# The attention softmax's scale moved into the query rows, its maximum written negated, and logits and transposes asked for one weight unit sooner

## The chip, the core and the metric

The kernel runs on one core of a Trainium2 chip. A core has a matrix engine (TensorE, PE in the profile, with its weight loads as PEld), two engines for rows of numbers (VectorE, DVE; ScalarE, ACT), GpSimd (POOL) and a queue that only starts transfers (SyncE, SP). They run side by side, each through its own list of instructions, and wait for each other by semaphores. PE writes into PSUM, a small memory of sums; the others work between PSUM and SBUF. The metric is the device time of one launch in microseconds (us), as the median of several runs.

## The reference

One layer of a streaming encoder over 256 rows of 2048 numbers, all in 32-bit floats: a feed-forward half step, a mixer, attention on 256 memory rows, a second feed-forward half step, a last norm. The change touches the attention alone:

```python
def mem_cross_attention(h, mem_h, w_q, w_kv, w_o):
    q = (h @ w_q).reshape(b, s, XATTN_HEADS, XATTN_HEAD_DIM)
    kv = (mem_h @ w_kv).reshape(b, mem_h.shape[1], 2, XATTN_HEADS, XATTN_HEAD_DIM)
    k, v = kv[:, :, 0], kv[:, :, 1]
    logits = jnp.einsum('bshd,bmhd->bhsm', q, k).astype(jnp.float32) * (XATTN_HEAD_DIM ** -0.5)
    p = jax.nn.softmax(logits, axis=-1).astype(v.dtype)
    o = jnp.einsum('bhsm,bmhd->bshd', p, v).reshape(b, s, D_MODEL)
    return o @ w_o
```

There are 4 heads of 512 columns. `h` and `mem_h` are the normed rows (each row by the root of its mean square, times a gain).

## The kernel before

**Numbers in two parts.** Every operand of a product is split into a high part in the format that PE multiplies (`fp32r`) and the rest: the high part is a cast on ACT, the low part a subtraction on DVE. A product is then three matmuls: high by high, high by low, low by high (`products`). Activations lie split in `xs` and `ys`.

**Weights stream.** Weights come from memory in units of 1 MB (a tile `raw`, three buffers, loaded on SP's queue at L627). ACT casts the high part `wh` (L1582), DVE subtracts the low part `wl` (L453; a share of some units goes to POOL, L457); each has three buffers. The class `Stream` holds the list of units with their matmuls. Before the matmuls of a unit it asks for the split of the unit two further on; the load of `raw` follows when the split of the third unit before it has given the buffer back. Other work is put between units with `st.op(f, after)`: `f` is asked for when `after` more units have been put in the list. A planner then sets the final order on each engine from its own idea of times, so an op that is asked for sooner is not always placed sooner.

**Blocks.** `block_s` makes 1024 columns for 256 rows from eight units. A plain unit is 24 matmuls of 512 columns (L362). Some units are taken in pairs of row and column halves with seven products in place of eight, 21 matmuls (`seven`, L507). For these the split is another: sums `T` of the weights on DVE (L486), their casts `wh` (L489) and rest `wl` (L453), and casts and rest `xh`, `xl` of the raw weights (L279, L280). The buffers of `T`, `xh` and `xl` are lent by other tiles of the stage (`homes`); in the key and value blocks `xh` and `xl` live in the tiles `att` and `kv`, and the latter is also the home of the split keys and values.

A block with seven-product units needs four tiles of sums in PSUM, and PSUM has just four (`psum`, `bufs=4`, two banks each): two for the whole sums, which every unit adds to, and two "parts" tiles for sums that only the seven-product units make, called A (first and sixth product) and B (seventh and fifth) here. In the profile all four are named `pt`, as are the tiles of the probabilities' transposes. At the last seven-product unit the parts are added up on ACT and DVE (`combine`, L574 to L579), at the block's end they go into the whole sums (L589).

**The attention stage.** Two blocks make the queries (`w_q`), and `ev_Q` multiplies the rows by the norm's factor `Rcol` on ACT before they are turned (`turn_Q`). Then twice, for two heads each: a block for the keys, turned and split by `turn_K`, and a block for the values. The unit order of a value block is (1, 5, 3, 0, 6, 4, 2, 7): the fourth, sixth and seventh unit are seven-product units, the others plain. The softmax of the two heads lies inside this value block:

- `logits(h)`: 24 matmuls into a PSUM tile `pl` (L1321), the rows' maximum on DVE (L1327), times minus the scale (L1328), for two halves of rows the exponential on ACT with its row sums (L1331), the reciprocal of the sums (L1335) and the scaling of the probabilities `P` by it (L1337), both on DVE.
- `probs(h)`: four transposes of `P` on PE into a PSUM tile (L1343), split into `PT` by ACT (L285) and DVE (L286).
- `values(h)`: at the block's end, 48 matmuls for two heads (L1360).

So while the value block holds its two whole sums, the other two PSUM tiles pass from the logits of the two heads to the two heads' transposes and then to A and B. The output projection (`into_x` with `w_o`) follows behind the second value block. The lines that ask for the softmax stand between the key block and the value block:

```python
        for j in (1, 0):
            h = 2 * b + j
            st.op(lambda h=h: turn_K(h), 1)
        for h in (2 * b, 2 * b + 1):
            st.op(lambda h=h: logits(h), 2)
            st.op(lambda h=h: probs(h), 3)
        block_s(wwide(w_kv, D + b * 2 * NB), xs, kv_sums, KV_ORDER, ev_V(b))
```

The functions that the change touches, with the line numbers of the profile:

Of the kernel before, what the change touches and what calls it, by code (L numbers as in the profile page):

```python
# [9 lines left out]
AF = mybir.ActivationFunctionType  # L10
ALU = mybir.AluOpType
AX = mybir.AxisListType
PSUM = bass.MemoryType.PSUM

P = 128
D = 2048
S = 256
M = 256
# [8 lines left out]
XHD = D // H  # L27
# [72 lines left out]
def build(ctx, tc, I, out):  # L100
    nc = tc.nc
    st = Stream()
# [34 lines left out]
    def ptile(name):  # L137
        return psum.tile([P, 2, NB], F32, tag="ps", name=name)
# [6 lines left out]
    def uid(s):  # L145
        cnt[0] += 1
        return f"{s}{cnt[0]}"
# [9 lines left out]
    def whole_lines(pool, shape, dt, tag, name, bufs=1):  # L157

        n = 1
        for s in shape[1:]:  # L160
            n *= s
        t = pool.tile([shape[0], -(-n // LINE) * LINE], dt, tag=tag, name=name, bufs=bufs)[:, :n]
        if len(shape) == 3:
            t = t.rearrange("p (a b) -> p a b", b=shape[2])
        elif len(shape) == 4:
            t = t.rearrange("p (a b c) -> p a b c", b=shape[2], c=shape[3])
        return t

    def ctl(name, shape):
        return whole_lines(const, shape, F32, name, name)  # L170
# [10 lines left out]
    Rcol = ctl("Rcol", [P, 2])  # L181
# [88 lines left out]
    def among_weights(f):  # L270


        scalar, vector = behind_weights(f)
        latest["vector"] = vector
        if scalar is not None:
            latest["scalar"] = scalar
# [7 lines left out]
    def split(hi, lo, src):  # L284
        high = nc.scalar.copy(hi, src)  # L285
        return high, nc.vector.tensor_tensor(out=lo, in0=src, in1=f32(hi), op=ALU.subtract)  # L286

    def split_pair(dst, kt, src):
        split(dst[:, kt : kt + 2, 0, :], dst[:, kt : kt + 2, 1, :], src)
# [349 lines left out]
    def wwide(w, n0, k0=0, nk=KT):  # L639

        def src(k):
            def load(raw):
                raw = raw.rearrange("p (k n) -> p k n", n=2 * NB)
                if len(loaded) < 3:
                    for kk in range(2):
                        parts = (0, NB) if not loaded else (0,)
                        for c in parts:
                            n = 2 * NB // len(parts)
                            wload(raw[:, kk : kk + 1, c : c + n], w, k + kk, 1, n0 + c, n)
                else:  # L650
                    wload(raw, w, k, 2, n0, 2 * NB)
                next(first_loads, None)
                loaded.append(1)
            return load
        return [src(k0 + k) for k in range(0, nk, 2)]
# [557 lines left out]
    for b in range(2):  # L1213
        block_b(wblock(w_in, (4 + b) * NB), xs, ev_v(b))
        for i in range(2):
            h = 2 * b + i
# [24 lines left out]
    xa = {}  # L1241

    def xt(name, shape, dt=F32, tag=None, bufs=1):
        t = whole_lines(scope["pool"], shape, dt, tag or name, uid(name), bufs)
        xa[name] = t
        return t
# [46 lines left out]
    def ev_Q(b):  # L1293
        def evict(j, c):
            for h in range(2):
                nc.scalar.activation(c[:, h, :], c[:, h, :], AF.Copy, scale=Rcol[:, h : h + 1])
            held["Q", b, j] = c
        return evict

# [4 lines left out]
    def turn_K(h):  # L1304
        v = rows_turned(held["K", h])
        K = xa["K", h] = xt("K", [P, 4, 2, M], F32R, tag="kv", bufs=2)
        split(K[:, :, 0, :], K[:, :, 1, :], v)

    def ev_V(b):
        def evict(j, c):  # L1310
            V = xa["V", 2 * b + j] = xt("V", [P, 2, 2, XHD], F32R, tag="kv", bufs=2)
            split(V[:, :, 0, :], V[:, :, 1, :], c)
        return evict

    def logits(h):
        ps = ptile(uid("pl"))
        for t in range(2):
            tok = slice(t * P, (t + 1) * P)
            parts = [(d, a, b) for d in range(4) for a, b in ((0, 0), (0, 1), (1, 0))]
            for i, (d, a, b) in enumerate(parts):  # L1320
                nc.tensor.matmul(  # L1321
                    ps[:, t, :M], ys[:, 4 * h + d, a, tok], xa["K", h][:, d, b, :],
                    start=i == 0, stop=i == 11,
                )
        scale = XHD ** -0.5
        nm, sm = xt("nm", [P, 2], bufs=2), xt("sm", [P, 2], bufs=2)
        nc.vector.tensor_reduce(out=nm, in_=ps[:, :, :M], axis=AX.X, op=ALU.max)  # L1327
        nc.vector.tensor_scalar_mul(nm, nm, -scale)  # L1328
        pr = xa["P", h] = xt("P", [P, 2, M], bufs=2)
        for t in range(2):  # L1330
            nc.scalar.activation(  # L1331
                pr[:, t, :], ps[:, t, :M], AF.Exp, scale=scale, bias=nm[:, t : t + 1],
                accum_out=sm[:, t : t + 1],
            )
        nc.vector.reciprocal(out=sm, in_=sm)  # L1335
        for t in range(2):
            nc.vector.tensor_scalar_mul(pr[:, t, :], pr[:, t, :], sm[:, t : t + 1])  # L1337

    def probs(h):
        ps = ptile(uid("pt"))  # L1340
        for mtile in range(2):
            for t in range(2):
                nc.tensor.transpose(  # L1343
                    ps[:, mtile, t * P : (t + 1) * P], xa["P", h][:, t, mtile * P : (mtile + 1) * P], ident
                )
        if h % 2 == 0:
            xt("PT", [P, D], F32R)
        PT = xa["PT", h] = xa["PT"][:, h % 2 * 4 * S : (h % 2 + 1) * 4 * S].rearrange(
            "p (m a s) -> p m a s", m=2, a=2
        )  # L1350
        split(PT[:, :, 0, :], PT[:, :, 1, :], ps[:, :, :S])

    def values(h):
        for p in range(2):
            ps = ptile(uid("pv"))
            for d in range(2):
                col = slice((2 * p + d) * P, (2 * p + d + 1) * P)
                parts = [(m, a, b) for m in range(2) for a, b in ((0, 0), (0, 1), (1, 0))]
                for i, (m, a, b) in enumerate(parts):
                    nc.tensor.matmul(  # L1360
                        ps[:, d, :S], xa["V", h][:, m, a, col], xa["PT", h][:, m, b, :],
                        start=i == 0, stop=i == 5,
                    )
            split_pair(ys, 4 * h + 2 * p, ps[:, :, :S])

    for g, after in zip(q_sums.pairs, (3, 7)):
        st.op(lambda g=g: among_weights(lambda: q_sums.make(g)), after)
    for b in range(2):
# [9 lines left out]
    for b in range(2):  # L1378
        block_s(wwide(w_kv, b * 2 * NB), xs, kv_sums, KV_ORDER if b else KEY_ORDER,
                lambda j, c, b=b: held.__setitem__(("K", 2 * b + j), c),  # L1380
                sevens=() if b else (0, 4))
        for j in (1, 0):
            h = 2 * b + j
            st.op(lambda h=h: turn_K(h), 1)
        for h in (2 * b, 2 * b + 1):
            st.op(lambda h=h: logits(h), 2)
            st.op(lambda h=h: probs(h), 3)
        block_s(wwide(w_kv, D + b * 2 * NB), xs, kv_sums, KV_ORDER, ev_V(b))
        for h in (2 * b, 2 * b + 1):
            st.op(lambda h=h: values(h), 1)  # L1390
# [211 lines left out]
def program(shapes):  # L1602
    import concourse.bacc as _bacc

    nc = _bacc.Bacc("TRN2", target_bir_lowering=False, num_devices=1)
    args = {
        name: nc.dram_tensor(f"in_{name}", shapes[name], F32, kind="ExternalInput").ap()
        for name in _INS
    }
    out = nc.dram_tensor("out", _OUT, F32, kind="ExternalOutput").ap()  # L1610
    with tile.TileContext(nc, schedule_with_timeline_sim=True) as tc, ExitStack() as ctx:
        build(ctx, tc, args, out)
    return nc
# [10 lines left out]
```

## Time and profile before

| | |
|---|---|
| runs | 2086.03, 2086.88, 2087.07 us; median 2086.88 |
| profiled execution | 2086.24 us, span of the trace 2084.1 us |
| granted TensorE clock | 0.999 |
| busy in the span | PE 2069.3, weight loads 1724.8, DVE 1800.0, ACT 1143.4, POOL 98.6 us |
| busy from 1100 to 1200 us | PE 98.50, DVE 83.02, ACT 52.15 us |
| busy from 1200 to 1300 us | PE 98.48, DVE 77.83, ACT 48.17 us |
| busy from 1300 to 1400 us | PE 100.00, DVE 83.48, ACT 57.31 us |
| logits' matmuls (L1321) | 96, first 1149.1, last 1255.8 us |
| probabilities' transposes (L1343) | 16, first 1161.5, last 1270.7 us |

How to read it. Matmuls overlap each other, and their ends are worked out by the profiler and not seen, so their durations (0.39 us for 512 columns) add up to more than the time that passes; what counts is the distance from one start to the next. In a time line, a row stands for one or more like instructions in a run, with the start of the first, the time to the end of the last, the engine, the line, the tile written and those read, and the count; in square brackets how long the engine stood idle before it and what ended that. In a list of waits, a row names the waiting engine, tile and line, what it waited for, and then the total in us, how many times, and the longest.

### The profile page before, as it was taken

How to read it: one execution, taken by the hardware profiler on the slowest of the kernel's cores; microseconds unless marked ns; L12 is line 12 of the kernel's file. 1: busy time of each engine (PE TensorE's matmuls, PEld its weight loads, DVE VectorE, ACT ScalarE, POOL GpSimd, SP SyncE). 2: the span in 40 equal slices, each digit the busy share in tenths (PEclk: the TensorE clock that was granted, in tenths of full speed). 3: DMA queues.
4: the chain of work that ended last, by engine and by line, in shares of the span. 5: the costliest groups of instructions: out<-in, count | busy, mean ns of one | idle time of the engine just before them, and what ended most of it. 6: DMA issues, size and time to landing. Idle time of an engine off the chain costs nothing.

```text
span 2084.1 us, 24353 instructions
## 1 busy us (share of the span) xinstructions
PE 2069.3 (99%) x9651; PEld 1724.8 (83%) x9651; DVE 1800.0 (86%) x1689; ACT 1143.4 (55%) x1136; POOL 98.6 (5%) x87
## 2 busy tenths in 40 slices
PE   9999999999999999999999999999999999999998
PEld 7888888888888888888888888888888888888886
DVE  7998899989998677679789787879988999889987
ACT  7655455645654545455755554556554556545554
POOL 0000000000000000000000000000100010000001
PEclk9999999999999999999999999999999999999999
DMA  7666666567656755467655455665576765676664
GB/s 264 208 200 229 232 222 222 182 222 243 223 200 221 245 164 185 159 192 275 220 181 189 155 182 172 211 224 202 182 241 207 240 206 196 222 238 227 208 228 150
DMA packets 131178, 435.95 MB, mean 209 GB/s; under 512 B 9844, under 2 KB 13528, under 8 KB 130680
## 3 DMA queue, kind: packets, MB, share of 16 engines
q1 hardware_dynamic: 130888, 433.86, 61.8%
q8 instruction: 76, 1.25, 0.2%
q10 hardware_dynamic: 176, 0.53, 0.1%
q14 instruction: 38, 0.31, 0.0%
HBM read 417.58 MB, written 16.78 MB: 208 GB/s over the span
## 4 chain that ended last, share of the span: by engine, by line
PE 98%; DVE 1%; ACT 0%; issue 0%; DMA 0%; SPq 0%; DVEq 0%; ACTq 0%
PE pt L362 58%; PE pt L507 27%; PE pa L347 6%; PE pb L362 2%; PE ph L780 1%; DVE wl L453 1%; PE pl L1321 1%; PE pv L1360 1%; PE px L791 1%; PE pp L1012 0%; PE pe L362 0%; DMA x<-in_x 0%; ACT wh L1582 0%; ACT wh L489 0%; PE pa L1039 0%
## 5 line engine op out<-in xcount | busy, mean ns | idle before, releaser
L362 PE MATMUL pt<-wh,xs 128*128 128x512 f32 x2080 | 666.6, 390 | 0.6 <-ACT xs L236 0.6
L453 DVE TENSOR_TENSOR wl<-raw,wh 128x2048 fp32r<-128x2048 f32 (+1 forms) x253 | 545.2, 2161 | 138.4 <-ACT wh L1582 138.0
L1582 ACT CAST wh<-raw 128x2048 fp32r<-128x2048 f32 x253 | 483.4, 1913 | 301.5 <-PE pt L362 126.7
L362 PE MATMUL pt<-wh,ys 128*128 128x512 f32 x1472 | 463.9, 389 | 0.0
L489 ACT CAST wh<-T 128x1024 fp32r<-128x1024 f32 x242 | 254.1, 1054 | 373.9 <-DVE T L486 361.6
L362 PEld LDWEIGHTS pt<-wh,xs 128*128 128x128 f32 x2080 | 389.8, 188 | 80.8 <-ACT xs L236 0.9
L362 PE MATMUL pt<-wl,xs 128*128 128x512 f32 x1040 | 405.4, 391 | 2.3 <-DVE wl L453 2.3
L362 PEld LDWEIGHTS pt<-wh,ys 128*128 128x128 f32 x1472 | 276.3, 188 | 57.0
L362 PE MATMUL pt<-wl,ys 128*128 128x512 f32 x736 | 286.7, 390 | 0.0
L453 DVE TENSOR_TENSOR wl<-T,wh 128x2048 fp32r<-128x2048 f32 (+1 forms) x121 | 271.6, 2245 | 2.9 <-ACT wh L489 2.6
L362 PEld LDWEIGHTS pt<-wl,xs 128*128 128x128 f32 x1040 | 195.3, 188 | 43.0 <-DVE wl L453 3.1
L280 DVE TENSOR_TENSOR xl<-raw,xh 128x1536 fp32r<-128x1536 f32 x121 | 211.9, 1752 | 13.7 <-ACT xh L279 13.5
L279 ACT CAST xh<-raw 128x1536 fp32r<-128x1536 f32 x121 | 179.0, 1480 | 54.9 <-PE pt L507 35.7
L486 DVE TENSOR_TENSOR T<-T,raw 128x512 f32<-128x512 f32 x242 | 167.0, 690 | 6.2
L362 PEld LDWEIGHTS pt<-wl,ys 128*128 128x128 f32 x736 | 138.2, 188 | 28.6
L486 DVE TENSOR_TENSOR T<-raw 128x1024 f32<-128x1024 f32 x121 | 147.5, 1219 | 0.5
L507 PE MATMUL pt<-wh,xs 128*128 128x512 f32 x376 | 145.8, 389 | 0.0
L507 PE MATMUL pt<-xh,xs 128*128 128x512 f32 x376 | 140.8, 390 | 0.0
L457 POOL TENSOR_TENSOR wl<-raw,wh 128x768 fp32r<-128x768 f32 x40 | 74.3, 1857 | 1380.0 <-DVE wl L453 1358.9
L347 PE MATMUL pa<-xs,wh 128*128 128x512 f32 x384 | 135.6, 397 | 0.0
L507 PE MATMUL pt<-wh,xe 128*128 128x512 f32 x320 | 124.3, 389 | 0.0
L347 PE MATMUL pa<-xs,wl 128*128 128x256 f32 x384 | 106.8, 282 | 0.0
(248 smaller groups left out, 2343.8 us busy)
## 6 DMA issues: line engine op xcount, KB each, us to landing
raw<-in_ffn_w_down SPq DMA_DIRECT2D x88, 1024.0 KB, 5.5
raw<-in_ffn_w_up SPq DMA_DIRECT2D x80, 1024.0 KB, 5.0
raw<-in_ffn_w_gate SPq DMA_DIRECT2D x77, 1024.0 KB, 5.0
raw<-in_w_in SPq DMA_DIRECT2D x32, 1024.0 KB, 5.2
raw<-in_xattn_w_kv SPq DMA_DIRECT2D x32, 1024.0 KB, 5.0
raw<-in_w_out SPq DMA_DIRECT2D x16, 1024.0 KB, 5.6
raw<-in_xattn_w_q SPq DMA_DIRECT2D x16, 1024.0 KB, 5.6
raw<-in_xattn_w_o SPq DMA_DIRECT2D x16, 1024.0 KB, 5.6
```

Of the source, the lines that this page charges most:

```text
L279: in_turn("scalar", lambda: nc.scalar.copy(hi, src))
L280: in_turn("vector", lambda: nc.vector.tensor_tensor(out=lo, in0=src, in1=f32(hi), op=ALU.subtract))
L347: nc.tensor.matmul(o, w, x, start=k == 0 and i == 0, stop=last and i == 1)
L362: nc.tensor.matmul(ps, a, w, start=first and i == 0, stop=last and i == 2)
L453: in_turn("vector", lambda: nc.vector.tensor_tensor(out=lo[:, :n], in0=src[:, :n], in1=f32(hi[:, :n]), op=ALU.subtract))
L457: rest = nc.gpsimd.tensor_tensor(out=lo[:, n:], in0=src[:, n:], in1=f32(hi[:, n:]), op=ALU.subtract)
L486: in_turn("vector", lambda: nc.vector.tensor_tensor(out=o, in0=a, in1=b, op=ALU.add))
L489: in_turn("scalar", lambda: nc.scalar.copy(th[:, c], t[:, c]))
L507: nc.tensor.matmul(banks[n], x, w, start=n in fresh and j == 0, stop=n in ends and j == 2)
L780: nc.tensor.transpose(v[:, i, h * P : (h + 1) * P], g[:, h, i * P : (i + 1) * P], ident)
L791: nc.tensor.transpose(v[:, j, h * P : (h + 1) * P], x[:, h, j * P : (j + 1) * P], ident)
L1582: in_turn("scalar", lambda: nc.scalar.copy(hi, raw))
```

## The change

Three edits in the attention stage.

- The scale of the softmax, 512 to the power of minus one half, goes into the query rows: a new op `query_factor`, asked for three units into the first query block, writes `Rq`, the norm's factor times the scale, with one product on DVE (128 x 2). `ev_Q` multiplies by `Rq` where it took `Rcol`. The exponentials take the logits unscaled.
- The reduce writes the negated maximum itself (`negate=True`), and the product that made it so is gone: one instruction of DVE for each of 4 heads.
- `logits` is asked for after one unit of the value block in place of two, `probs` after two in place of three.

```diff
     def ev_Q(b):
         def evict(j, c):
             for h in range(2):
-                nc.scalar.activation(c[:, h, :], c[:, h, :], AF.Copy, scale=Rcol[:, h : h + 1])
+                nc.scalar.activation(c[:, h, :], c[:, h, :], AF.Copy, scale=xa["Rq"][:, h : h + 1])
             held["Q", b, j] = c
...
-        scale = XHD ** -0.5
         nm, sm = xt("nm", [P, 2], bufs=2), xt("sm", [P, 2], bufs=2)
-        nc.vector.tensor_reduce(out=nm, in_=ps[:, :, :M], axis=AX.X, op=ALU.max)
-        nc.vector.tensor_scalar_mul(nm, nm, -scale)
+        nc.vector.tensor_reduce(out=nm, in_=ps[:, :, :M], axis=AX.X, op=ALU.max, negate=True)
         pr = xa["P", h] = xt("P", [P, 2, M], bufs=2)
         for t in range(2):
             nc.scalar.activation(
-                pr[:, t, :], ps[:, t, :M], AF.Exp, scale=scale, bias=nm[:, t : t + 1],
+                pr[:, t, :], ps[:, t, :M], AF.Exp, bias=nm[:, t : t + 1],
                 accum_out=sm[:, t : t + 1],
             )
...
+    def query_factor():
+        xt("Rq", [P, 2])
+        nc.vector.tensor_scalar_mul(xa["Rq"], Rcol, XHD ** -0.5)
+
+    st.op(query_factor, 3)
...
         for h in (2 * b, 2 * b + 1):
-            st.op(lambda h=h: logits(h), 2)
-            st.op(lambda h=h: probs(h), 3)
+            st.op(lambda h=h: logits(h), 1)
+            st.op(lambda h=h: probs(h), 2)
```

In the order of instructions that the planner makes of the changed program, the logits' matmuls stand where they stood among the value block's matmuls. On ACT the exponentials of the second head stand ahead of the sixth unit's two casts `wh` (L489), where they stood behind them; on DVE the reciprocal and the scaling of `P` of the second head stand ahead of the sixth unit's `wl`, and both heads' `PT` ahead of the seventh unit's `xl`, where the second head's stood behind the seventh unit's `wl`. On PE the second head's four transposes stand together in the fifth unit; before, they stood one and three, among the products of the sixth and fourth unit with A. The matmuls of the fourth and the sixth unit with B follow there, ahead of the seventh unit's. On SP a fetch of the old `x` (L746) stands behind one weight load of the output projection that it stood ahead of. The line numbers of the changed program are up to 3 higher from L1366 on, and 1 to 2 lower from L1326 to L1360.

## The prediction

> **What bounds the kernel now.** I read the page first, then the waits of TensorE, then the time lines of four engines around the attention steps. The page: the span, the busy shares, and the engine shares of the chain that ended last.
>
> ```profile
> span 2084.1 us, 24353 instructions
> PE 2069.3 (99%) x9651; PEld 1724.8 (83%) x9651; DVE 1800.0 (86%) x1689; ACT 1143.4 (55%) x1136; POOL 98.6 (5%) x87
> PE 98%; DVE 1%; ACT 0%; issue 0%; DMA 0%; SPq 0%; DVEq 0%; ACTq 0%
> ```
>
> TensorE (PE) is the path: 98% of the chain. No matmul is taken away, so all that can be won is time in which PE stands still. The waits of PE from 1100 to 1560 us, the whole cross-attention from the value projection on (total us, times, longest):
>
> ```profile
> PE pt L362 <- DVE wl L453: 2.3, 2, 1.2
> PE pt L507 <- DVE wl L453: 0.6, 2, 0.3
> ```
>
> Everything comes twice: once in each value block, two heads each, near 1175 and 1275 us. PE's time line of the second one (start, us, tile out<-in, count, idle before):
>
> ```profile
> 1261.55 0.60 PE L1343 MATMUL pt<-ident,P 128*128 128x128 f32 x4
> 1261.90 0.48 PE L362 MATMUL pt<-wl,xs 128*128 128x512 f32 x1
> ...
> 1268.39 0.39 PE L507 MATMUL pt<-wh,xs 128*128 128x512 f32 x1
> 1268.62 0.27 PE L1343 MATMUL pt<-ident,P 128*128 128x128 f32 x1
> 1268.64 0.48 PE L507 MATMUL pt<-xh,xs 128*128 128x512 f32 x1
> 1268.96 0.40 PE L507 MATMUL pt<-xl,xs 128*128 128x512 f32 x1
> ...
> 1270.56 0.49 PE L1343 MATMUL pt<-ident,P 128*128 128x128 f32 x3
> 1270.81 0.48 PE L507 MATMUL pt<-xh,xs 128*128 128x512 f32 x1
> ...
> 1272.28 0.39 PE L507 MATMUL pt<-xh,ye 128*128 128x512 f32 x1
> 1272.71 0.50 PE L507 MATMUL pt<-xl,xs 128*128 128x512 f32 x1
> 1273.05 0.40 PE L507 MATMUL pt<-xh,xs 128*128 128x512 f32 x1
> ...
> 1274.43 0.39 PE L507 MATMUL pt<-wh,xs 128*128 128x512 f32 x1
> 1275.14 0.50 PE L507 MATMUL pt<-wl,ye 128*128 128x512 f32 x1 [0.32 <-DVE wl L453]
> 1275.49 0.40 PE L507 MATMUL pt<-wh,ye 128*128 128x512 f32 x1
> ...
> 1277.35 0.40 PE L507 MATMUL pt<-wh,ye 128*128 128x512 f32 x1
> ...
> 1280.31 0.61 PE L362 MATMUL pt<-wh,xs 128*128 128x512 f32 x2
> 1282.07 0.50 PE L362 MATMUL pt<-wl,xs 128*128 128x512 f32 x1 [1.15 <-DVE wl L453]
> 1282.41 0.63 PE L362 MATMUL pt<-wh,xs 128*128 128x512 f32 x2
> ...
> 1287.19 0.39 PE L362 MATMUL pt<-wh,ys 128*128 128x512 f32 x1
> ```
>
> The reader is to look at starts, not at durations, which overlap. From 1277.35 to 1280.31 stand 13 matmuls: 0.228 us from start to start, the undisturbed step. Above it are three stalls: 1272.28 to 1272.71 (0.20 over the step), 1274.43 to 1275.14 (0.48) and 1280.31 to 1282.07 (1.76 for two steps, 1.30 over). The step behind each is long too (0.34, 0.35, 0.34: 0.11, 0.12, 0.11 over). Sum 2.32 us. After each group of transposes the first matmul takes 0.32 (1268.64 to 1268.96), 0.09 over.
>
> Why they arise: VectorE (DVE), then ScalarE (ACT), same stretch.
>
> ```profile
> 1256.28 0.69 DVE L1327 TENSOR_REDUCE nm<-pl 128x2 f32<-128x512 f32 x1 [0.26 <-PE pl L1321]
> ...
> 1257.41 1.75 DVE L280 TENSOR_TENSOR xl<-raw,xh 128x1536 fp32r<-128x1536 f32 x1
> 1259.08 0.17 DVE L1328 TENSOR_SCALAR nm<-nm 128x2 f32<-128x2 f32 x1
> ...
> 1265.44 0.61 DVE L1337 TENSOR_SCALAR P<-P,sm 128x256 f32<-128x256 f32 x2
> ...
> 1270.90 1.76 DVE L280 TENSOR_TENSOR xl<-raw,xh 128x1536 fp32r<-128x1536 f32 x1 [4.25 <-ACT xh L279]
> 1272.80 2.29 DVE L453 TENSOR_TENSOR wl<-T,wh 128x2048 fp32r<-128x2048 f32 x1
> 1275.01 0.69 DVE L286 TENSOR_TENSOR PT<-pt,PT 128x512 fp32r<-128x512 f32 x1
> 1279.73 3.69 DVE L453 TENSOR_TENSOR wl<-raw,wh 128x2048 fp32r<-128x2048 f32 x2 [4.04 <-ACT wh L1582]
> ```
>
> ```profile
> 1260.70 0.47 ACT L1331 ACTIVATE P<-pl,nm 128x256 f32<-128x256 f32 x1
> ...
> 1269.39 1.48 ACT L279 CAST xh<-raw 128x1536 fp32r<-128x1536 f32 x1 [6.61 <-PE pt L507]
> 1270.78 1.99 ACT L489 CAST wh<-T 128x1024 fp32r<-128x1024 f32 x2
> 1277.78 3.71 ACT L1582 CAST wh<-raw 128x2048 fp32r<-128x2048 f32 x2 [4.54 <-PE pt L507]
> ```
>
> PSUM holds four tiles: the block's two whole sums, and two that pass from the logits of two heads to the transposes of their probabilities and then to the two parts tiles, A and B, of the seven-product units. The second head's transposes (1268.62 and 1270.56) are read out last by DVE at 1275.01, so B opens at 1275.7. Until then PE can only work on A and the whole sums, and runs into the seventh unit's xl (ready 1272.66) and wl (ready 1275.09): the two short stalls. The fourth unit's wh, which B needs as well, is given back after B's product at 1277.35; only then does ACT cast the eighth unit (1277.78, idle 4.54 for it), DVE subtracts at 1279.73 (idle 4.04), and PE waits until 1282.07: the long stall. So the second head's softmax is late, and neither DVE nor ACT is short of time.
>
> **The change part by part.** In the changed program's order the logits stand where they stood: they follow the key tiles' splits. What moves is behind them.
>
> (1) The second head. Its two exponentials stand ahead of the sixth unit's wh casts instead of behind them, and its reciprocal and two scalings ahead of that unit's wl. Its transposes form one group of four in the fifth unit, ten matmuls behind the first head's group, which itself goes three matmuls sooner. By the rows: the first group starts three steps before 1261.55, at 1260.87; four transposes take 0.35 (1261.55 to 1261.90), then come 0.09 and ten steps: the second group starts at 1263.6 in place of 1268.62. Its P: where the reduce starts now, 1256.28, the first head's two scalings (0.61) go first and end at 1256.9, the reduce (0.69) at 1257.6, the two exponentials (0.47 each, 0.20 to read out each sum) by 1258.9, xl (1.75) at 1259.3, reciprocal and scalings (0.17 and 0.61) at 1260.1. Margin 3.5 us. Both heads' PT are then copied by ACT behind the second group and subtracted by DVE (0.69 each, with T's sums between) by about 1266, so A and B are open when PE reaches them: 1268.62 plus the 0.44 of the second group is 1269.1, and B seven steps on, 1270.7.
>
> (2) What is late next. The fourth unit's products with B now precede the seventh unit's. Of the second group, 0.35+0.09 falls before the xh cast instead of 0.02+0.09 of the single transpose, so that cast starts at 1269.7 (before 1269.39), wh follows to 1273.1, xl ends 1273.0, wl 1275.4. The eighth unit's wh buffer comes free ten matmuls after the row that starts the xh cast, near 1272.2; ACT casts from 1273.0, DVE's wl ends near 1277.6. PE, without a stall, gets to the seventh unit's xl 28 matmuls after 1269.05, at 1275.4, to its wl at 1277.5 and to the eighth unit's wl at 1279.7. The margins are 2.4, 2.1 and 2.1 us. So all three stalls go: 2.32 a pair.
>
> (3) Three groups of transposes become two: 0.09 a pair. The eight transposes stay.
>
> (4) The four negating products (0.17 each at 1259.08) leave DVE; they lay in DVE's wait for wh and count nothing by themselves. The reduce with negation has no row: between nothing and a second pass of its own 0.69; I take nothing, the nearest row being the plain reduce, and the 3.5 us of (1) cover the upper end. An exponential without scale: the 0.47 row, with nothing to 0.17 either way, under the same cover.
>
> (5) The factor for the query rows: one more 128x2 product.
>
> ```profile
> 1005.14 0.17 DVE L224 RECIPROCAL Rcol<-chain 128x2 f32<-128x2 f32 x1
> 1006.58 1.66 DVE L240 SCALAR_TENSOR_TENSOR xs<-px,gains,xs 128x256 fp32r<-128x256 f32 x4 [1.27 <-ACT xs L248]
> ```
>
> It goes between these two, 0.17 into 1.27 idle: nothing; 0.17 if that cover were gone. The scaling of the query rows reads another column, the same instruction.
>
> (6) Queues. On SP one fetch of the old x goes behind a weight load, and that load waits for the eighth unit's wl, which now ends 4 us sooner; the fetched x is wanted only in the output projection, from 1287.19 on and there after its products. On ACT, in the first value block, the delay is visible:
>
> ```profile
> 1157.19 0.20 ACT L1331 ACTIVATION_READ_ACCUMULATOR P<-pl,nm 128x1 f32 x1
> ...
> 1158.98 2.00 ACT L489 CAST wh<-T 128x1024 fp32r<-128x1024 f32 x2 [1.59 <-PE pt L362]
> ```
>
> The first head is done at 1157.4; reciprocal, scalings and reduce (0.17, 0.61, 0.69) bring the second head's exponentials to 1158.9, their end to 1160.2 at most: wh starts up to 1.2 late, so its wl (2.00, then 2.29) ends near 1164.5, and PE wants it at about 1168.8, the second block's 1268.8 less the 100 us between the blocks. Hidden by 4.3 us. POOL's share of the split keeps its place and follows its unit.
>
> Sum: 2 x (2.32 + 0.09) = 4.8 us. The profiled execution took 2086.24 us (span 2084.1), the median run 2086.88, 0.64 more; from the median, 2082.0 us (0.23% less).
>
> [...]
>
> **The rivals.** (a) The long stall stays: the eighth unit's wh gets its buffer from a later unit, or its load is late. It needs 2.1 us of delay, some ten matmuls. Then only 2 x (0.31 + 0.60 + 0.09) = 2.0 are won: 2084.9. Against it: the order puts the fourth unit's last use ten matmuls behind the row that frees xh.
>
> (b) The transposes do not decide, DVE's work does: 4 x 0.17 = 0.7 won, 2086.2. For it: the profile names DVE in all four waits, and DVE is 86% busy. Against it: its idle 4.04 right there.
>
> (c) Slower. PE takes its work in order, so the second head's transposes, then at 1263.6, stop PE if P is not there, and nothing hides that. Place: the fifth unit, twice. If P came as late as in the trace of before (exponentials from 1260.70, scalings ended by 1266.1), PE would wait 2.4 a pair, which eats the gain; from there each us costs 2.0, and 2.1 us more (P at 1268.2) gives 2091.1. Against it: P stands ready 3.5 us ahead. For it: one queue each on ACT and DVE, where the second head's work waits behind the first's. [...]
>
> **How the numbers follow.** Forecast 0.70, (a) 0.16, (b) 0.09, (c) 0.05. The forecast's own range is 2081.0 to 2083.0: the 0.09s and 0.17s, and runs that lie 2086.03 to 2087.07. Up to (a) it is 2081.0 to 2085.1, which leaves out (b) and (c). 0.2% of this time is 4.2 us, about what a measurement can tell from no change; the forecast lies 0.6 beyond it, so 0.03 of its 0.70 counts as the same. Faster 0.67, same 0.28, slower 0.05.
>
> **What would show it.** In the profile of after: no wait of PE for wl from 1150 to 1300; two groups of four transposes ten matmuls apart; in the second block, which comes 2.4 sooner, ACT's casts of the eighth unit near 1270.6 (1273.0 less 2.4) and not at 1277.78, and DVE's PT both ended by 1264; the output projection's first matmul near 1282.4 instead of 1287.19 (both pairs). A wait of PE before the second group shows (c); a wait of the eighth unit's wl shows (a). Wrong altogether would be a new wait in the blocks behind, where the freed 2.4 us a pair let PE run into a weight load.

## The result and the profile after

| | before | after |
|---|---|---|
| median of 11 runs | 2086.78 us (2086.03 to 2087.58) | 2081.48 us (2081.22 to 2082.50) |
| profiled execution, its span | 2086.24, 2084.1 us | 2082.50, 2080.3 us |

After over before is 0.9976, with a 95% interval from 0.9967 to 0.9985: 5.3 us faster. The forecast was 2082.0 us.

The profiled execution of after is the slowest of its eleven runs. The waits of PE over its whole span show where it lost time:

```profile
PE px L717 <- DMA x<-in_x: 1.8, 1, 1.8
PE pwarm L206 <- POOL ident masks.py:199: 1.4, 1, 1.4
```

These two rows are all the waits that the list still has. The first is for a load of `x` near the program's start. It is 1.8 us here and 0.5 us in the execution shown of before. The row that opens the attention stage's arithmetic on the queries shows by how much in all (DVE's time line, after; before it starts at 1005.14, quoted in step 5 of the prediction):

```profile
1006.39 0.17 DVE L224 RECIPROCAL Rcol<-chain 128x2 f32<-128x2 f32 x1
1006.59 0.17 DVE L1366 TENSOR_SCALAR Rq<-Rcol 128x2 f32<-128x2 f32 x1
1007.83 0.48 DVE L240 SCALAR_TENSOR_TENSOR xs<-px,gains,xs 128x256 fp32r<-128x256 f32 x1 [1.07 <-ACT xs L248]
```

So times of after are 1.25 us late against those of before, and 1.25 is to be taken off when they are compared. The page of after, the same three lines as before:

```profile
span 2080.3 us, 24347 instructions
...
PE 2067.9 (99%) x9651; PEld 1726.1 (83%) x9651; DVE 1800.3 (87%) x1686; ACT 1143.5 (55%) x1136; POOL 98.6 (5%) x87
...
PE 99%; DMA 0%; DVE 0%; ACT 0%; SPq 0%; DVEq 0%; issue 0%; ACTq 0%
```

DVE's 1% of the chain is gone. PE's time line of the second value block:

```profile
1259.62 0.60 PE L1341 MATMUL pt<-ident,P 128*128 128x128 f32 x4
1259.97 0.47 PE L362 MATMUL pt<-wl,xs 128*128 128x512 f32 x1
...
1262.35 0.60 PE L1341 MATMUL pt<-ident,P 128*128 128x128 f32 x4
1262.70 0.71 PE L362 MATMUL pt<-wh,xs 128*128 128x512 f32 x2
...
1270.53 0.39 PE L507 MATMUL pt<-wh,ye 128*128 128x512 f32 x1
...
1274.15 0.39 PE L507 MATMUL pt<-xl,xs 128*128 128x512 f32 x1
...
1276.19 0.39 PE L507 MATMUL pt<-wl,xs 128*128 128x512 f32 x1
...
1278.46 0.39 PE L362 MATMUL pt<-wl,xs 128*128 128x512 f32 x1
...
1283.45 0.39 PE L362 MATMUL pt<-wh,ys 128*128 128x512 f32 x1
```

No row carries a wait. The row at 1270.53 is the fourth unit's last product with B (1277.35 before); 1274.15, 1276.19 and 1278.46 are the first uses of the seventh unit's `xl` and `wl` and of the eighth unit's `wl`, the three places where PE stood still. The last row is the output projection's first matmul. From the reciprocal to it pass 277.06 us (1283.45 - 1006.39), before 282.05 (1287.19 - 1005.14): 4.99 us less, in the stretch in which the forecast's sum put 4.8. What feeds these uses, DVE and then ACT:

```profile
1257.77 0.62 DVE L1335 TENSOR_SCALAR P<-P,sm 128x256 f32<-128x256 f32 x2
...
1262.92 0.69 DVE L286 TENSOR_TENSOR PT<-pt,PT 128x512 fp32r<-128x512 f32 x1
...
1264.12 0.69 DVE L286 TENSOR_TENSOR PT<-pt,PT 128x512 fp32r<-128x512 f32 x1
...
1269.97 1.76 DVE L280 TENSOR_TENSOR xl<-raw,xh 128x1536 fp32r<-128x1536 f32 x1 [4.56 <-ACT xh L279]
1271.87 2.29 DVE L453 TENSOR_TENSOR wl<-T,wh 128x2048 fp32r<-128x2048 f32 x1
1274.08 3.69 DVE L453 TENSOR_TENSOR wl<-raw,wh 128x2048 fp32r<-128x2048 f32 x2
```

```profile
1268.46 1.48 ACT L279 CAST xh<-raw 128x1536 fp32r<-128x1536 f32 x1 [4.89 <-PE pt L507]
1269.84 2.00 ACT L489 CAST wh<-T 128x1024 fp32r<-128x1024 f32 x2
1271.74 3.72 ACT L1585 CAST wh<-raw 128x2048 fp32r<-128x2048 f32 x2
```

Both engines now go from the seventh unit into the eighth without a pause: the idle 4.54 and 4.04 us that stood in these rows before are gone. `xl` ends at 1271.7, `wl` at 1274.2 and the eighth unit's `wl` at 1276.4 (1274.08 + 2.29), while PE asks at 1274.15, 1276.19 and 1278.46: margins of 2.4, 2.0 and 2.1 us.

### The profile page after: what moved, and what is told of

Read it like the earlier page. It is cut to its first block, busy times and chain, and to the rows that moved or that the text cites. A ratio compares the mean times of both kernels' runs of the same rounds, so it can differ in the third digit from the quotient of the medians.

```text
span 2080.3 us, 24347 instructions
## 1 busy us (share of the span) xinstructions
PE 2067.9 (99%) x9651; PEld 1726.1 (83%) x9651; DVE 1800.3 (87%) x1686; ACT 1143.5 (55%) x1136; POOL 98.6 (5%) x87
## 3 DMA queue, kind: packets, MB, share of 16 engines
q8 instruction: 76, 1.25, 0.2%
## 4 chain that ended last, share of the span: by engine, by line
PE 99%; DMA 0%; DVE 0%; ACT 0%; SPq 0%; DVEq 0%; issue 0%; ACTq 0%
PE pt L362 58%; PE pt L507 28%; PE pa L347 7%; PE pb L362 2%; PE ph L780 1%; PE pl L1321 1%; PE pv L1358 1%; PE px L791 1%; DMA x<-in_x 0%; PE pp L1012 0%; PE pe L362 0%; PE pa L1039 0%; PE po L1161 0%; PE tm L1268 0%; PE px L717 0%; PE pq L1148 0%
## 5 line engine op out<-in xcount | busy, mean ns | idle before, releaser
L489 ACT CAST wh<-T 128x1024 fp32r<-128x1024 f32 x242 | 254.1, 1055 | 368.5 <-DVE T L486 358.8
```

The lines of the kernel that those rows point to most:

```text
L489: in_turn("scalar", lambda: nc.scalar.copy(th[:, c], t[:, c]))
```

## The experiments

The result leaves three things open: which of the edits moved the order, whether the removed DVE work has any part in the gain, and what in the order costs the time. I call three theories O (the order alone counts), S (asking one unit sooner is what does it) and R (DVE's saved work does).

Two numbers describe the order of each kernel, counted on PE's list of matmuls and transposes behind a pair's last logits matmul: where the groups of transposes stand, and how many matmuls lie between the first seven-product unit's last product with B (which gives back the `wh` buffer that the eighth unit waits for) and the eighth unit's first product with `wl`. This second number is called the distance. By the rows of before it has to cover 4.7 us: from 1277.35 over the cast at 1277.78 and the subtraction behind it to 1282.07, which is 21 steps of 0.228. No kernel below has a distance between 15 and 30, so the 21 is worked out and not measured.

| kernel | transposes | distance | median, us |
|---|---|---|---|
| before | 4 at 24, 1 at 57, 3 at 66 | 15 | 2086.78 |
| after | 4 at 21, 4 at 35 | 35 | 2081.48 |
| 1 arithmetic alone | 4 at 21, 4 at 35 | 35 | 2081.59 |
| 2 asked sooner alone | 4 at 24, 1 at 57, 3 at 66 | 15 | 2086.45 |
| 3 negation apart | 4 at 24, 1 at 57, 3 at 66 | 15 | 2085.98 |
| 4 idle products on DVE | 4 at 21, 4 at 36 | 35 | 2081.31 |
| 5 second head at the end | 4 at 21, 4 at 126 | 38 | 2081.65 |
| 6 exponentials three times | 4 at 33, 4 at 57 | 30 | 2081.62 |
| 7 idle reduces on DVE | 4 at 21, 1 at 41, 3 at 43 | 30 | 2081.47 |
| 8 query block's order | 4 at 21, 4 at 35 | 35 | 2080.76 |
| 9 before, other unit order | 4 at 43, 4 at 48 | 30 | 2082.95 |
| 10 after, other unit order | 4 at 21, 1 at 48, 3 at 59 | 15 | 2086.09 |
| 11 negation on ACT | 8 at 32 | 34 | 2081.18 |
| 12 both 8 and 11 | 8 at 32 | 34 | 2079.92 |

The kernel before had medians of 2086.70 beside experiments 1 to 4, 2086.77 beside 5 to 8, 2086.54 beside 9 to 11 and 2086.28 beside 12. Each other median is of 6 to 11 runs.

### Which edit moves the order: experiments 1 to 3

**1, the arithmetic alone.**

```diff
-            st.op(lambda h=h: logits(h), 1)
-            st.op(lambda h=h: probs(h), 2)
+            st.op(lambda h=h: logits(h), 2)
+            st.op(lambda h=h: probs(h), 3)
```

> The changed kernel with logits and probs asked for after two and three units, as before the change: only the arithmetic is new. Theory O (the place of the second head's transposes decides, and the planner moves them because the negating product has left DVE's queue): the order on PE is that of the changed kernel, two groups of four transposes ten matmuls apart, so 2081.5 us and no wait of PE for wl between 1150 and 1300 us. Rival S (asking one unit sooner is what moves them): 2086.8 us with the 2.9 us of waits of before. Rival R (the 0.17 us products that DVE is spared count by themselves, 4 x 0.17 = 0.7): 2086.1 us.

Measured: 2081.59 us, 0.9976 of before (0.9966 to 0.9985). No wait of PE from 1000 to 1560 us.

**2, asked sooner alone.** The diff against the kernel before:

```diff
-            st.op(lambda h=h: logits(h), 2)
-            st.op(lambda h=h: probs(h), 3)
+            st.op(lambda h=h: logits(h), 1)
+            st.op(lambda h=h: probs(h), 2)
```

> The kernel before with logits and probs asked for one unit sooner, its arithmetic untouched. Theory O: the order on PE is that of before (transposes four, then one and three), so 2086.8 us and PE's waits for wl are all back, 2.9 us in 4 waits. Rival S: 2081.5 us, no such wait. Rival R: 2086.8 us too, since DVE has all its products.

Measured: 2086.45 us, 0.9999 (0.9990 to 1.0008). S is out: asking sooner moves nothing, and without it the whole gain is there.

**3, the negation as a product of its own.** Against the changed kernel:

```diff
-        nc.vector.tensor_reduce(out=nm, in_=ps[:, :, :M], axis=AX.X, op=ALU.max, negate=True)
+        nc.vector.tensor_reduce(out=nm, in_=ps[:, :, :M], axis=AX.X, op=ALU.max)
+        nc.vector.tensor_scalar_mul(nm, nm, -1.0)
```

> The changed kernel (scale in the query rows, asked for one unit sooner), but the negation is a product of its own again, by -1, on DVE. Theory O: with the product back in DVE's queue the planner's order is that of before, so 2086.8 us and the 2.9 us of waits. Rival S: 2081.5 us, since all else of the change is there. A rival by which the exponential without scale saves time: four heads, two exponentials each, so 2081.5 to 2086.8 by as much as each is shorter than 0.47 us.

Measured: 2085.98 us, 0.9997 (0.9988 to 1.0006). The waits of PE from 1000 to 1560 us in this kernel, and the place of its transposes:

```profile
PE pt L362 <- DVE wl L453: 2.3, 2, 1.2
PE pt L507 <- DVE wl L453: 0.6, 2, 0.3
```

```profile
1261.42 0.60 PE L1342 MATMUL pt<-ident,P 128*128 128x128 f32 x4
1268.45 0.27 PE L1342 MATMUL pt<-ident,P 128*128 128x128 f32 x1
1270.40 0.49 PE L1342 MATMUL pt<-ident,P 128*128 128x128 f32 x3
```

To the tenth of a microsecond that the list shows, the waits of before are back, and the transposes stand one and three again. So one instruction of 0.17 us on DVE, for each head, decides which of two orders the planner writes; what in the planner tips is not shown. The scale in the query rows, which this kernel still has, gains nothing by itself: it lets that instruction go.

### Whether DVE's work counts: experiments 4, 7 and 11

**4, idle products.** Against the changed kernel, behind the scaling of `P`:

```diff
+        for _ in range(4):
+            nc.vector.tensor_scalar_mul(nm, nm, 1.0)
```

> The changed kernel with four idle products (128x2, about 0.17 us each) on DVE behind the scaling of P of every head, which nothing reads: 16 x 0.17 = 2.7 us more work on DVE than after the change, and 2.0 us more than before it. The order on PE stays that of the changed kernel but for one matmul (the second group of transposes eleven matmuls behind the first). Theory O: the second head's P has 4 us to spare, of which 0.7 goes, so 2081.5 us and no wait of PE for wl. Rival R (DVE's work decides): 2.0 us over the kernel before, 2088.8 us, or at least the 0.7 us of the change lost.

Measured: 2081.31 us, 0.9975 (0.9966 to 0.9984), no wait of PE in the value blocks.

**7, idle reduces,** at the same place:

```diff
+        for _ in range(4):
+            nc.vector.tensor_reduce(out=nm, in_=pr, axis=AX.X, op=ALU.max)
```

> The changed kernel with four idle reduces of P (128x512 from SBUF, some 0.3 to 0.7 us each) on DVE behind the scaling of P of every head: 5 to 11 us more work on DVE. The second head's transposes stand 16 to 18 matmuls behind the first head's (10 in the changed kernel). Theory O: B opens 1.6 us later, within the margin of 2.1 us, so 2081.5 to 2082.5 us. Rival R (DVE's work decides): 5 us or more over the changed kernel, 2086.5 us or more.

Measured: 2081.47 us, 0.9975 (0.9965 to 0.9984). The group of the added reduces on DVE, with its total and the mean of one, and the page's busy times:

```profile
L1337 DVE TENSOR_REDUCE nm<-P 128x2 f32<-128x512 f32 x16 | 10.7, 680 | 0.1
```

```profile
PE 2068.5 (99%) x9651; PEld 1726.8 (83%) x9651; DVE 1809.7 (87%) x1702; ACT 1143.9 (55%) x1136; POOL 98.6 (5%) x87
```

The added reduces take 10.7 us, fifteen times the 0.7 us that the change took away (DVE's busy time in all goes from 1800.3 to 1809.7 us). They stand right among the softmax's steps, and the time is the same. R is out.

**11, the negation on ACT.** The kernel before with one line changed:

```diff
-        nc.vector.tensor_scalar_mul(nm, nm, -scale)
+        nc.scalar.activation(nm, nm, AF.Copy, scale=-scale)
```

> The kernel before with the product that negates and scales the maximum moved from DVE to ACT (AF.Copy with a scale), asked for after two and three units as before: nothing is removed. In its order all eight transposes of a pair stand in one group, 8 matmuls behind the place of the first head's in the kernel before, and the first seven-product unit's last product with B 34 matmuls ahead of the eighth unit's first product with wl. Theory O: no stall, and one re-entry of 0.09 less a pair than the changed kernel: 2081.3 us. Rival R, in the form that the removed instruction counts: 2086.8 us, or more by the four products on ACT.

Measured: 2081.18 us, 0.9974 (0.9964 to 0.9984). Nothing is removed or folded. The four products stay between the reduce and the exponentials and even take a little longer than DVE's 0.17 us (group of lines, ACT, mean in ns behind the comma):

```profile
L1328 ACT ACTIVATE nm<-nm 128x2 f32<-128x2 f32 x4 | 0.8, 202 | 1.8 <-DVE nm L1327 1.8
```

and the whole gain is there, with all eight transposes in a single run on PE's time line:

```profile
1260.63 1.03 PE L1343 MATMUL pt<-ident,P 128*128 128x128 f32 x8
```

### What in the order costs the time: experiments 5, 6, 9 and 10

**5, the second head's transposes behind the value block.** Against the changed kernel:

```diff
-            st.op(lambda h=h: probs(h), 2)
+            st.op(lambda h=h: probs(h), 2 if h % 2 == 0 else 4)
```

> The changed kernel with the odd head's probs asked for after four units. In its order the second head's transposes stand 101 matmuls behind the first head's, behind the whole value block, and the tile of its logits passes straight to B, which opens as soon as the exponentials have read them. Theory O, in the form that the early release of B counts and not the transposes: 2081.5 us, no wait of PE for wl from 1150 to 1300 us. Rival (late transposes cost by themselves, as they seem to in the kernel before, where they stand 33 to 37 behind): 2086.8 us or more.

Measured: 2081.65 us, 0.9976 (0.9967 to 0.9985). PE's time line, and ACT's row of the eighth unit's cast:

```profile
1258.92 0.60 PE L1341 MATMUL pt<-ident,P 128*128 128x128 f32 x4
...
1282.28 0.60 PE L1341 MATMUL pt<-ident,P 128*128 128x128 f32 x4
```

```profile
1269.10 1.92 ACT L1585 CAST wh<-raw 128x2048 fp32r<-128x2048 f32 x1 [0.90 <-PE pt L507]
```

The second head is 23 us behind the first, later than in any other kernel here, and nothing is lost. By its order B takes over the tile of this head's logits, and the eighth unit's cast, which waits for a product with B, starts at 1269.10.

**6, every exponential three times.** Against the changed kernel:

```diff
                 accum_out=sm[:, t : t + 1],
             )
+            for _ in range(2):
+                nc.scalar.activation(
+                    pr[:, t, :], ps[:, t, :M], AF.Exp, bias=nm[:, t : t + 1],
+                    accum_out=sm[:, t : t + 1],
+                )
```

> The changed kernel with every exponential done three times (16 x 2 more of about 0.47 us on ACT, 7.5 us in all, of them 1.9 us per head). In its order the first head's transposes stand 12 matmuls later than in the changed kernel, and the second head's in one group where the kernel before has the first of its two pieces. The fourth unit's last product with B then stands 18 matmuls behind this group, near 1273.0 us in the second block, and the seventh unit's casts on ACT end at about the same time. Theory O in that form: the eighth unit's cast starts at 1273 and the margins of about 2 us hold, 2081.5 to 2082.5 us. Rival (it is the time of the second head's transposes that counts): the stalls are back, 2086 us or more. Rival (ACT's work): up to 7.5 us more than the changed kernel.

Measured: 2081.62 us, 0.9976 (0.9967 to 0.9985). The second group stands at position 57, where before had the first of its two pieces, and PE has no wait in the value block, at a distance of 30. The fourth unit's last product with B, the eighth unit's cast and subtraction, and the first product with its `wl` (PE, ACT, DVE, PE):

```profile
1270.32 0.39 PE L507 MATMUL pt<-wh,ye 128*128 128x512 f32 x1
```

```profile
1270.75 3.73 ACT L1590 CAST wh<-raw 128x2048 fp32r<-128x2048 f32 x2 [0.25 <-PE pt L507]
```

```profile
1272.74 3.69 DVE L453 TENSOR_TENSOR wl<-raw,wh 128x2048 fp32r<-128x2048 f32 x2
```

```profile
1277.12 0.39 PE L362 MATMUL pt<-wl,xs 128*128 128x512 f32 x1
```

ACT stands idle until this product gives the buffer back and casts 0.43 us behind its start. The first of the two `wl`, which takes 2.29 us, is ready at 1275.03, 4.7 us behind the product, as in before. But PE gets there 6.8 us behind it, so 2.1 us are to spare, as forecast. (This run's second block lies 2.6 us ahead of before's, so the 1273 of the forecast is 1270.4 here.) Late transposes as such are no cause. What differs is when B's tile is read out: here DVE reads the second head's transposes at 1267.25, ahead of the seventh unit's `xl`; in before it read them at 1275.01, behind that unit's `wl`. ACT's 7.8 us more, from sixteen added exponentials with sixteen reads of their sums, count nothing either (the page's busy times):

```profile
PE 2067.8 (99%) x9651; PEld 1725.9 (83%) x9651; DVE 1800.6 (87%) x1686; ACT 1151.3 (55%) x1168; POOL 98.6 (5%) x87
```

**9 and 10, the same other unit order in the kernel before and in the changed one.** One line in each:

```diff
-        block_s(wwide(w_kv, D + b * 2 * NB), xs, kv_sums, KV_ORDER, ev_V(b))
+        block_s(wwide(w_kv, D + b * 2 * NB), xs, kv_sums, (1, 5, 3, 6, 0, 4, 2, 7), ev_V(b))
```

> The kernel before, its arithmetic and its asking times untouched, with the unit order of the second value block of each pair set to (1, 5, 3, 6, 0, 4, 2, 7): one more plain unit ahead of the first of the three seven-product units. In its order the first seven-product unit's last product with B stands 30 matmuls ahead of the eighth unit's first product with wl (15 in the kernel before, 35 in the changed one). Theory O, sized by the rows: from that product to wl take about 4.7 us (cast, subtraction and hand-over), which 30 steps of 0.228 cover, 15 do not; so no long stall and about 2081.5 to 2082.5 us although nothing of the change is in it. Rival R or S (the arithmetic or the asking is what gains): 2086.8 us.

> The changed kernel, all of the change in it, with the same other unit order of the value block. In its order the second head's transposes stand one and three again, and the first seven-product unit's last product with B 15 matmuls ahead of the eighth unit's first product with wl. Theory O: 4.7 - 15 x 0.228 = 1.3 us of long stall a pair and the short ones as in the kernel before, so 2085 to 2087 us although it has all of the change, 3 to 5 us slower than the same unit order without the change. Rival R or S: 2081.5 us.

Measured: 2082.95 us for 9 (0.9985 of before, 0.9976 to 0.9994) and 2086.09 us for 10 (0.9998, 0.9989 to 1.0006). With these units the kernel before is the faster one, and the kernel with all of the change in it shows the old waits (10, waits of PE from 1000 to 1560 us, and the place of the long one on PE's time line):

```profile
PE pt L362 <- DVE wl L453: 2.4, 2, 1.2
PE pt L507 <- DVE wl L453: 0.6, 2, 0.3
```

```profile
1280.53 0.61 PE L362 MATMUL pt<-wh,xs 128*128 128x512 f32 x2
1282.35 0.50 PE L362 MATMUL pt<-wl,xs 128*128 128x512 f32 x1 [1.20 <-DVE wl L453]
```

Two steps take 1.82 us, 1.36 over, where the distance of 15 gave 1.3. Number 9 came out 0.5 us above the range that I had written down. It has no wait for `wl`; a new one takes its place (waits, and PE's time line):

```profile
PE pt L507 <- DVE PT L286: 1.5, 2, 0.7
```

```profile
1266.71 0.60 PE L1343 MATMUL pt<-ident,P 128*128 128x128 f32 x4
1268.05 0.50 PE L507 MATMUL pt<-xh,xs 128*128 128x512 f32 x1 [0.73 <-DVE PT L286]
```

The transposes stand directly ahead of a product with a parts tile, which needs the tile that DVE is still reading. The 1.5 us, with 0.11 for the slow step behind each, leave 2081.2. This is the price of the four tiles of the pool `psum` (`bufs=4`) seen from the other side: it is not the transposes that cost here, but the matmul right behind them that wants their tile.

### A better kernel: experiments 8 and 12

**8, the second query block's unit order.** The changed kernel still has four slow steps in this block (PE's time line, each row and the start behind it):

```profile
1067.42 0.39 PE L507 MATMUL pt<-wh,xs 128*128 128x512 f32 x1
1067.78 0.50 PE L507 MATMUL pt<-xl,xs 128*128 128x512 f32 x1
1068.11 0.40 PE L507 MATMUL pt<-xh,xs 128*128 128x512 f32 x1
...
1069.72 0.47 PE L362 MATMUL pt<-wh,xs 128*128 128x512 f32 x1
1070.26 0.49 PE L507 MATMUL pt<-wl,xs 128*128 128x512 f32 x1
1070.59 0.39 PE L507 MATMUL pt<-wh,xs 128*128 128x512 f32 x1
```

One place in `Q_ORDER` is changed, against the changed kernel:

```diff
-                                                        (0, 1, 4, 2, 5, 3, 6, 7))
+                                                        (0, 1, 4, 2, 3, 5, 6, 7))
```

> The changed kernel with the unit order of the second query block (0, 1, 4, 2, 3, 5, 6, 7) in place of (0, 1, 4, 2, 5, 3, 6, 7), so that one more plain unit stands between its two seven-product units. After the change this block holds the last stall that the trace shows inside the attention stage: four steps of 355, 337, 540 and 332 ns near 1067 us, 0.66 us over the step of 227. If it is the nearness of the two units (xh waits for the buffer that the first one holds): 2080.8 us. If the wait only moves to the next unit: 2081.5 us.

Measured: 2080.76 us, 0.9974 (0.9964 to 0.9983). No step of its time line between 1062 and 1075 us is over 0.23 us. The 0.7 us below the changed kernel are less than the intervals can tell, but they fit the four steps (0.66 us), which are gone from the time line.

**12, this order and the negation on ACT of experiment 11.**

> The two best orders together: the negating product on ACT (all else of the attention as before, asked for as before, eight transposes in one group) and the unit order (0, 1, 4, 2, 3, 5, 6, 7) of the second query block. If the two gains add: the 2081.2 us of the first less the 0.7 us that the query order gave the changed kernel, 2080.5 us, with no step of PE over 0.33 us between 860 and 1500 us. If the query order's gain hangs on the changed arithmetic: 2081.2 us.

Measured: 2079.92 us, 0.9968 (0.9956 to 0.9980), the fastest of all, 6.4 us below the kernel before run beside it. PE's waits over the whole span are the two at the start alone (1.4 us for `ident`, 0.4 for `x`), and between 1255 and 1265 us, where the eight transposes lie, no step is over 0.32 us. This fits two gains that add, although it came out 0.6 below the 2080.5. The kernel before was 0.26 faster beside it than beside experiment 11 (2086.28 to 2086.54); the other 0.3 its six runs do not settle. The wait for the load of `x` at the start alone differs by more than that between profiled executions: 0.4 us here, 1.8 in after.

## Why the prediction was right, and where its reason was too narrow

- **What bounds the kernel:** right. The three stalls a pair, 2.32 us each time, were the gain. Taking away 10.7 us of cover on DVE changed nothing (7), and orders with the old distance brought back every wait (2, 3, 10).
- **Step 1, the second head.** Places and margin as forecast: two groups of four, the second 14 positions behind the first's start. `P` is ready at 1258.4 and its transposes start at 1262.35, 4.0 us of margin (3.5 forecast). DVE's two `PT` end at 1264.8, less the shift 1263.6 (forecast: by 1264).
- **Step 2, what is late next.** Margins of 2.4, 2.0 and 2.1 us where 2.4, 2.1 and 2.1 were worked out; the eighth unit's cast at 1271.74, less the shift 1270.5 (forecast 1270.6); the output projection's first matmul at 1283.45, less the shift 1282.2 (forecast 1282.4). Nothing came late in place of the old stalls.
- **Step 3, one re-entry of 0.09 less a pair:** two rows of it are left (1259.97 and 1262.70), so that much went as forecast. But the term left out that the eight transposes themselves take longer in two groups: 0.70 us (1259.62 to 1259.97, 1262.35 to 1262.70) against 0.62 in before (0.35, 0.02 and 0.25 by the prediction's rows). The 0.09 and the 0.08 cancel, so this step is worth nothing. Eight in one group (11) do no better than two groups of four: 0.79 us and 0.09 against 0.70 and twice 0.09.
- **The sum:** that it came so near is in part luck. The stalls make 4.7 of the 4.99 us. The rest, some 0.15 a pair, lies in ordinary steps: in the second block 37 of them took 229 to 250 ns in before and 16 in after, where the undisturbed step takes 227.
- **Step 4, the reduce with negation.** It had no row, and its bounds were nothing and 0.69. The groups of lines of before and of after settle it:

```profile
L1327 DVE TENSOR_REDUCE nm<-pl 128x2 f32<-128x512 f32 x4 | 2.7, 687 | 1.1 <-PE pl L1321 1.1
```

```profile
L1326 DVE TENSOR_REDUCE nm<-pl 128x2 f32<-128x512 f32 x4 | 2.8, 688 | 0.9 <-PE pl L1321 0.9
```

  687 ns without and 688 with it: nothing. The exponentials, with the scale (before) and without it (after), 468 and 470 ns:

```profile
L1331 ACT ACTIVATE P<-pl,nm 128x256 f32<-128x256 f32 x8 | 3.7, 468 | 0.0
```

```profile
L1329 ACT ACTIVATE P<-pl,nm 128x256 f32<-128x256 f32 x8 | 3.7, 470 | 3.0 <-DVE nm L1326 3.0
```
- **Step 5:** `Rq` at 1006.59 lies in the idle time, which fell from 1.27 to 1.07 us. Nothing, as said.
- **Step 6:** in the first value block PE has no wait. The sixth unit's casts on ACT start there at 1161.03, less the shift 1159.8, so 0.8 us later than before (up to 1.2 forecast), and that stayed hidden.
- **The rivals.** (a) would have left waits for the eighth unit's `wl`; there are none. (b) is refuted by experiments 4, 7 and 11. (c) had its condition (the second head's transposes early, P late) unmet by 4.0 us. That PE takes its work in order, on which its price rests, shows in before: PE stood idle 1.15 us for the eighth unit's `wl` (1282.07), although the next matmuls, at 1282.41, take the same unit's `wh`, whose cast had ended by 1279.7 (1277.78 and 1.9). No run made P late enough to try its price, so that remains argued.

What the forecast had too narrow is the cause. It said that the second head's softmax is late, and took the softmax's place for the reason. In experiment 5 it is later still, and in 6 its transposes stand where before had the first of its two pieces, both at full speed; 7 has them in two pieces, one and three, and loses nothing by it. The long stall hangs on the place where the first seven-product unit's products with B stand: at a distance of 30 or more from the eighth unit's `wl` it is gone in ten kernels, at 15 it is there in all four. The two short stalls came and went with it, and no run parts them from it. In those four kernels DVE reads the second head's transposes out behind the seventh unit's `wl`, which holds B up; in nine others it does so ahead of that unit's `xl`, and in 5 behind the whole block, where B does not need their tile. Why the planner puts these products where it does is not shown. Nor did the forecast say which edit moves the order. It read the order and priced it, which was enough for the number; only experiments 1 to 3 and 11 show that a product of 0.17 us in DVE's queue tips it, and that the asking does nothing, alone (2) or on top (1).

## What to carry to other kernels

Where a planner writes the order, a small edit is worth what the new order is worth: read the order, find the wait that ends last at each place, and count the steps between the release of a buffer and the use of what is made in it. Here 4.7 us of cast and subtraction are 21 matmuls of cover at the measured 0.228 us a step, an estimate, and the one count told apart the kernels with the long stall (15) and without it (30 or more), whatever arithmetic they had; a count near 21 was not tried. When such an edit wins, undo its parts one at a time before the credit is given: the part named as the cause may do nothing, and a cheaper edit (one line that moves a product to another engine) may do it all.

## What the runs showed of the hardware that I had not expected

- Negation in the reduce and the scale in the exponential are free on these shapes: 688 against 687 ns, 468 against 470 ns.
- DVE took 5.4 us more work in each of two stretches of some 11 us (half of the 10.7 us, in experiment 7), with 87% of busy time over the whole span, and PE lost nothing: the idle time ahead of the seventh unit's `xl` was room (4.56 us in after, 1.07 in experiment 7), in spite of the share.
- ACT's product on 128x2 numbers takes 202 ns, DVE's 0.17 us (the row at 1259.08 of before), and the kernel with the slower one is 5.4 us faster.
